# A list-scheduled two-layer backbone: attention products bound into groups, new crossing times for the planner, and one Hyena block moved ahead of the first heads

## The chip, the cores and the metric

The kernel runs on one core of a Trainium2 chip. The metric is device time in microseconds of one execution, as the median over several runs. A separate profiled execution gives the trace that is quoted here.

## The reference

Two layers act on 512 latent and 256 context tokens of width 1024. Each layer is a half-step SwiGLU feed-forward, a token mixing, and a second half-step feed-forward, with layer norms and a modulation computed from the conditioning vectors.

```python
def token_mix(h_lat, h_ctx, w_in, w_out, ...):
    p_lat = h_lat @ w_in
    p_ctx = h_ctx @ w_in
    ...
    oa_l = block_attention(qa_l, concat([ka_c, ka_l]), concat([va_c, va_l]), HEAD_DIM ** -0.5)
    ...
    oc_l = block_attention(qc_l, concat([kc_c, kc_l]), concat([vc_c, vc_l]), (C_NOPE + C_ROPE) ** -0.5)
    ob_l = hyena_mix(pb_l, *hy)
    out_lat = concat([oa_l, ob_l, oc_l]) @ w_out
```

Group A is a grouped-query attention (6 query heads, 2 key heads, width 64), group C a latent attention (6 heads), group B a Hyena convolution with 256 channels. Latent queries read 256 context and 512 latent keys, context queries read context keys. Layer 0 also needs the context outputs, layer 1 only the latent ones.

## The kernel before

**A program that is recorded and then ordered.** The code does not issue instructions directly. A `Recorder` stands in for the engines: `record` notes each operation with its dependencies (from the regions of tiles that it reads and writes), its tiles and a planned `cost`. `order` then runs a list scheduler over all of them: for each of the engines it keeps the operations whose inputs will be there, always takes the engine that can start first, and on it the available operation that comes first in the program. Tile buffers from rotating pools (22 units, 13 weight tiles, 8 banks of PSUM) are handed out in this simulated time too. The result is one fixed order for each engine; on the chip the engines only wait for semaphores. Every instruction of the trace therefore carries one line, L324 (`issue`), and is told apart by tiles and shapes.

**The planner's constants.** `LAT` is what it adds between an operation's planned end and the start of one that depends on it: on the same engine, on another engine, when TensorE is one of the two, and after a DMA. `cost` holds formulas for the duration on each engine. TensorE is also planned at double cost for `WARM` ns after an idle time of more than `IDLE`.

**One step of an attention.** `attend` runs over blocks of 128 queries for two heads at once. It computes scores into PSUM (banks S for the latent keys, C for the context keys), takes row maxima on VectorE, exponentials on ScalarE, sums and a division on VectorE, transposes the weights on TensorE (`turn`), copies the transposes to SBUF on ScalarE (T[0] for the latent keys in two copies, one for each head, then T[1] for the context keys in one) and multiplies values with them. The last part reads

```python
            for i, (k, t, w, c) in enumerate(at):
                for r in range(2):
                    nc.tensor.matmul(o[64 * r:64 * r + 64], vals(h0 + r, k), t[:, w * r + c:w * r + c + 128],
                                     start=i == 0, stop=i == len(at) - 1, tile_position=(0, 64 * r))
```

so that the two heads (r = 0 and 1) fill the two column halves of the array in turn. All of a step's products write one bank `o`, and each one depends on the one before. A latent block has 6 key tiles and so 12 products, a context block 2 key tiles and 4 products. In the trace a product is two recorded matmuls of the form `128*64 128x128`. Layer 0 runs 6 query blocks for 3 pairs of heads in each of the two attentions, layer 1 runs 4. Nothing in the recorder says that a step's products belong together.

**Projections between the heads.** `mix` projects keys, values and queries, transposes them, and splits queries into a high and a low part on ScalarE and VectorE (the `u<-p,u` differences). Then `weave` interleaves the steps of attention A (`heads_a`) with `hy_proj`, a generator that yields after each projection of one Hyena weight block: 24 matmuls for the latent tokens, and in layer 0 as many for the context. A block is followed by a short convolution, one activation on ScalarE and two steps on VectorE (`t<-p,convw,t`) that read the PSUM bank. There are 6 weight blocks. `weave` emits the first block after the first head step; since position in the program is the scheduler's priority, this decides who goes first on each engine where both could go. The weights of a block come by DMA from `in_w_hy` and are split into two parts (`w<-raw` on ScalarE, `w<-raw,w` on VectorE). After attention A follow the Hyena transform, attention C with its own projections woven in, and the output projection.

Of the kernel before, what the change touches and what calls it, by code (L numbers as in the profile page):

```python
# [49 lines left out]
class Recorder:  # L50
# [6 lines left out]
    WRITES = ("out", "accum_out")  # L57
    AHEAD = {"p": 100, "w": 12}
    IDLE, WARM = 3200.0, 3400.0
    LAT = {"same": 130.0, "cross": 180.0, "tensor": 270.0, "dma": 3000.0}  # L60

    def __init__(self, nc):
        self.nc = nc
        self.ops = []
        self.touch, self.first = {}, {}
        self.pools = {}
        for e in ("tensor", "vector", "scalar", "gpsimd", "sync"):
            setattr(self, e, _Engine(self, e))

# [38 lines left out]
    def record(self, eng, method, args, kw):  # L108
# [30 lines left out]
                self.touch[name] = keep  # L139
        self.ops.append((eng, method, args, kw, deps, tiles, self.cost(eng, method, args, kw)))  # L140

    @staticmethod
    def cost(eng, method, args, kw):

        out = args[0]
        n = 1
        for d in out.shape[1:]:
            n *= d
        if eng == "sync":
            b = 4 * n * out.shape[0]  # L150
            return 60.0 + b / 340.0
        if eng == "tensor":
            if method == "transpose":
                return 107.0
            if args[1].dtype != F32:
                return 13.0 + (1.0 if n >= 256 else 4.0) * n / 2.4
            return 13.0 + 4.0 * n / 2.4 * (0.3 if args[1].shape[-1] == 64 and n <= 128 else
                                           min(1.0, args[1].shape[-1] / 128.0))
        ins = [x for x in args[1:] if isinstance(x, bass.AP)]
        psum = any(x.space == PSUM for x in ins)  # L160
        for x in ins:
            m = 1
            for d in x.shape[1:]:
                m *= d
            n = max(n, m)
        small = sum(isinstance(x, bass.AP) for k, x in kw.items() if k in ("bias", "scale", "accum_out"))
        small += sum(isinstance(x, bass.AP) and x.shape[-1] == 1 for x in args[2:])
        if eng == "scalar":
            return (90.0 if not psum else 52.0) + 93.0 * small + 0.833 * n
        if eng == "gpsimd":  # L170
            if method == "tensor_copy":
                return 150.0 + 3.0 * n
            return 130.0 + (3.5 if method == "tensor_scalar" else 2.13) * n
        if method == "reciprocal":
            return 65.0 + 6.3 * n
        fast = method in ("tensor_scalar", "tensor_copy", "memset") and not psum
        return 68.0 + 62.0 * small + (0.52 if fast else 1.04) * n
# [13 lines left out]
    def order(self):  # L191
        ops = self.ops
# [37 lines left out]
        avail = {e: [] for e in when}  # L230
        res = []
        quiet, cold = -1e9, 0.0
        port = {"vector": 0.0, "gpsimd": 0.0}
        shares = [self.shares(*op[:4]) for op in ops]
        starts = self.starts = [0.0] * N

        def offer(n):

            t0 = ready[n]
            for tag, r in opens[n]:  # L240
                if not slots[tag].safe(r):
                    slots[tag].parked[r] = n
                    return
                t0 = max(t0, slots[tag].free[0])
            heapq.heappush(future[ops[n][0]], (t0, n))
# [4 lines left out]
        while len(res) < N:  # L250
            best = None
            for e in when:
                while future[e] and future[e][0][0] <= when[e]:
                    heapq.heappush(avail[e], heapq.heappop(future[e])[1])
                if avail[e]:
                    t0 = when[e]
                elif future[e]:
                    t0 = future[e][0][0]
                else:
                    continue  # L260
                if best is None or t0 < best[0]:
                    best = (t0, e)
            t0, e = best
            when[e] = t0
            while future[e] and future[e][0][0] <= t0:
                heapq.heappush(avail[e], heapq.heappop(future[e])[1])
            n = heapq.heappop(avail[e])
            if shares[n]:
                free = port["gpsimd" if e == "vector" else "vector"]
                if free > t0 + 60.0:  # L270

                    passed = [n]
                    while avail[e] and len(passed) < 12 and shares[avail[e][0]]:
                        passed.append(heapq.heappop(avail[e]))
                    m = heapq.heappop(avail[e]) if avail[e] and not shares[avail[e][0]] else None
                    for x in passed[m is None:]:
                        heapq.heappush(avail[e], x)
                    if m is not None:
                        n = m
            if any(not slots[tag].safe(r) or slots[tag].free[0] > t0 for tag, r in opens[n]):  # L280
                offer(n)
                continue
            wake = []
            for tag, r in opens[n]:
                slots[tag].take(r)
                wake.append(tag)
            res.append(n)
            if shares[n]:
                t0 = max(t0, port["gpsimd" if e == "vector" else "vector"])
                port[e] = t0 + ops[n][6]  # L290
            starts[n] = t0
            end = t0 + ops[n][6]
            if e == "tensor":
                if t0 - quiet > self.IDLE:
                    cold = t0 + self.WARM
                if t0 < cold:
                    end += ops[n][6]
                quiet = end
            when[e] = end
            done = end + (self.LAT["dma"] if e == "sync" else 0.0)  # L300
            for m in succ[n]:
                f = ops[m][0]
                lat = 0.0 if e == f == "tensor" else self.LAT["same" if e == f else "tensor" if "tensor" in (e, f) else "cross"]
                ready[m] = max(ready[m], done + lat)
                need[m] -= 1
                if not need[m]:
                    offer(m)
            for t in ops[n][5]:
                left[t] -= 1
                ends[t] = max(ends.get(t, 0.0), done)  # L310
                if not left[t] and self.pools.get(t) in slots:
                    tag = self.pools[t]
                    slots[tag].give(rank[t], ends[t] + self.LAT["cross"])
                    wake.append(tag)
            for tag in wake:
                for m in slots[tag].woken():
                    offer(m)
# [9 lines left out]
def weave(main, n, side, m):  # L327

    done = 0
    for i, _ in enumerate(main, 1):  # L330
        while done * n < i * m and done < m:
            next(side, None)
            done += 1
    for _ in side:
        pass
# [45 lines left out]
class Core:  # L381
# [617 lines left out]
    def mix(self, l, need_ctx):  # L999
        nc, a, tc = self.nc, self.a, self.tc  # L1000
# [3 lines left out]
        nq = len(qtoks)  # L1004
        streams = ((0, NLT), (NLT, NT)) if need_ctx else ((0, NLT),)
# [74 lines left out]
        for j0, j1 in both:  # L1080
            n = 128 * (j1 - j0)
# [59 lines left out]
        for j0, j1 in streams:  # L1141
            n = 128 * (j1 - j0)
# [64 lines left out]
        def heads_a():  # L1207
            for hp in range(3):
                kept.append(self.unit())
                yield from self.attend(score_a, lambda h, j: Vj(j, 64 * (h // 3), 64 * (h // 3) + 64), 2 * hp, qtoks,  # L1210
                                       hp, kept[hp])

        weave(heads_a(), 3 * nq, hy_proj(), 6 * len(streams))
        for hp in range(3):
            n = 128 * nq
            self.split(self.H[:, hp, :n], self.Hl[:, hp, :n], kept[hp][:, :n])
# [98 lines left out]
        ops = []  # L1315
# [7 lines left out]
    def attend(self, score, vals, h0, qtoks, kt, keep=None):  # L1323

        nc = self.nc
        tt = nc.vector.tensor_tensor
        for j in qtoks:
# [7 lines left out]
            m, z, y = self.small(4), self.small(4), self.small(2)  # L1335
# [30 lines left out]
                turn(p[:, 256 * r:256 * r + 256], r, 512)  # L1366
            nc.scalar.copy(T[1][:, 0:512], p)
            o = self.ps()[:, :128]
            at = [(i, T[0], 512, 128 * i) for i in range(NLT)] if lat else []
            at += [(NLT + i, T[1], 256, 128 * i) for i in range(NT - NLT)]  # L1370
            for i, (k, t, w, c) in enumerate(at):
                for r in range(2):
                    nc.tensor.matmul(o[64 * r:64 * r + 64], vals(h0 + r, k), t[:, w * r + c:w * r + c + 128],
                                     start=i == 0, stop=i == len(at) - 1, tile_position=(0, 64 * r))
            jj = slice(128 * j, 128 * j + 128)
            if keep is None:
                self.split(self.H[:, kt, jj], self.Hl[:, kt, jj], o)
# [259 lines left out]
```

## Time and profile before

| | us |
|---|---|
| median of 3 runs | 2939.81 |
| lowest, highest | 2936.02, 2941.83 |
| the profiled execution | 2944.45 |
| its span, first to last instruction | 2942.3 |
| TensorE busy in it | 2842.6 |

The profiled execution has its own time, which lies a little above the runs' median; its trace is read against that time. Its mean granted TensorE clock is 0.984 of full speed. A matmul's recorded end is modelled and matmuls overlap, so the time that one costs is read from its start to the start of the next. In the timelines, consecutive instructions of one form are merged into one row with their count.

### The profile page before, as it was taken

Reading aid. Unit: us, or ns where it says so; the run is one execution under the profiler, and the core shown is the slowest. Engines: PE = TensorE matmul, PEld = TensorE weight load, DVE = VectorE, ACT = ScalarE, POOL = GpSimd, SP = SyncE. Lnnn points to the kernel's source line nnn. Section 1 sums busy time; section 2 is a strip of 40 time slices with the busy share of each in tenths; the row PEclk is TensorE's granted clock in tenths of the full one; section 3 lists DMA queues with packets and bytes.
Section 4 is the critical chain, followed back from the end, with each engine's and each line's share of the span. In section 5 each row is a group of like instructions: output and inputs, shape, how many; then the busy total and the mean of one; then the engine's idle time right before and its main releaser. Section 6 shows DMA issues by size and latency. Waiting matters only on the chain.

```text
span 2942.3 us, 41183 instructions
## 1 busy us (share of the span) xinstructions
PE 2842.6 (97%) x16132; PEld 2429.0 (83%) x16132; DVE 1713.4 (58%) x3485; ACT 1012.1 (34%) x1988; POOL 558.9 (19%) x545
## 2 busy tenths in 40 slices
PE   7999999999998999999999899999999899799998
PEld 5888888878887799888888788888889687688886
DVE  7887666377577572656536863653267666623335
ACT  4222121255556552121222421212217557432221
POOL 3201223024020031012211220122115120110220
PEclk9999999999999999999999899999999999999999
DMA  8654443122021303343321441431212112123231
GB/s 280 229 158 147 133 136 111 53 90 69 27 68 37 101 30 101 115 129 122 108 93 41 136 143 65 126 101 65 79 63 101 34 58 87 58 87 113 94 107 66
DMA packets 105714, 291.36 MB, mean 99 GB/s; under 512 B 15184, under 2 KB 17392, under 8 KB 105520
## 3 DMA queue, kind: packets, MB, share of 16 engines
q1 hardware_dynamic: 105520, 288.73, 30.3%
q8 instruction: 127, 2.08, 0.3%
q14 instruction: 67, 0.55, 0.1%
HBM read 277.23 MB, written 11.45 MB: 98 GB/s over the span
## 4 chain that ended last, share of the span: by engine, by line
PE 60%; DVE 5%; ACT 2%; issue 1%; POOL 0%; DVEq 0%; ACTq 0%
PE p L324 60%; DVE u L324 2%; DVE s L324 2%; ACT t L324 1%; DVE w L324 1%; DVE t L324 1%; ACT u L324 0%; ACT Hhi L324 0%; ACT w L324 0%; POOL Hlo L324 0%; DVE junk L324 0%; DVE adaw L324 0%; DVE Hlo L324 0%; ACT L324 0%; DVEq L1633 0%
## 5 line engine op out<-in xcount | busy, mean ns | idle before, releaser
L324 PE MATMUL p<-Hhi,w 128*128 128x256 f32 (+1 forms) x5536 | 1367.3, 337 | 8.1 <-ACT Hhi L324 6.1
L324 PEld LDWEIGHTS p<-Hhi,w 128*128 128x128 f32 x5536 | 953.8, 191 | 123.7 <-issue 7.0
L324 PE MATMUL p<-Hlo,w 128*128 128x256 f32 (+1 forms) x2768 | 930.3, 336 | 0.5 <-POOL Hlo L324 0.5
L324 PE MATMUL p<-w,u 128*128 128x512 f32 x2904 | 665.8, 390 | 0.0
L324 PEld LDWEIGHTS p<-w,u 128*128 128x128 f32 x2904 | 543.5, 188 | 111.9
L324 DVE TENSOR_TENSOR w<-raw,w 128x1024 fp32r<-128x1024 f32 (+2 forms) x312 | 389.5, 1249 | 423.1 <-PE p L324 337.6
L324 PEld LDWEIGHTS p<-Hlo,w 128*128 128x128 f32 x2768 | 527.2, 191 | 54.1 <-issue 1.2
L324 ACT CAST w<-raw 128x1024 fp32r<-128x1024 f32 (+2 forms) x312 | 323.0, 1043 | 723.1 <-PE p L324 648.7
L324 POOL TENSOR_TENSOR u<-t,u 128x512 fp32r<-128x512 f32 (+1 forms) x154 | 181.2, 1177 | 1260.3 <-ACT u L324 1141.8
L324 PE MATMUL p<-u,u 128*64 128x128 f32 (+7 forms) x2120 | 299.4, 330 | 20.9 <-ACT t L324 6.1
L324 DVE TENSOR_TENSOR t<-t,p 128x512 f32<-128x512 f32 (+1 forms) x160 | 90.9, 568 | 387.4 <-PE p L324 355.2
L324 PEld LDWEIGHTS p<-u,u 128*64 128x64 f32 (+4 forms) x2120 | 212.3, 162 | 83.7 <-issue 35.7
L324 POOL TENSOR_TENSOR u<-u,t 128x512 f32<-128x512 f32 (+2 forms) x128 | 160.5, 1281 | 524.3 <-DVE t L324 416.0
L324 DVE SCALAR_TENSOR_TENSOR junk<-adaw,crow 128x512 bf16<-128x512 f32 x256 | 207.8, 812 | 74.0 <-PE p L324 46.4
L324 ACT CAST u<-t 128x512 fp32r<-128x512 f32 (+1 forms) x154 | 81.3, 528 | 424.6 <-DVE t L324 424.6
L324 DVE SCALAR_TENSOR_TENSOR adaw<-adaw,crow 128x512 f32<-128x512 f32 x256 | 212.0, 828 | 6.8
L324 PE MATMUL p<-w,Hhi 128*128 128x512 f32 (+3 forms) x712 | 193.8, 355 | 6.9 <-ACT w L324 6.9
L324 DVE TENSOR_TENSOR t<-p,u 128x512 f32<-128x512 f32 x196 | 131.6, 686 | 94.8 <-PE p L324 92.1
L324 ACT ACTIVATE t<-p 128x512 f32<-128x512 f32 (+2 forms) x162 | 79.9, 495 | 293.2 <-PE p L324 287.9
L324 PE MATMUL p<-ident,t 128*128 128x128 f32 x848 | 127.3, 285 | 32.1 <-ACT t L324 17.3
L324 ACT COPY u<-p 128x512 f32<-128x512 f32 (+4 forms) x225 | 112.3, 530 | 94.9 <-PE p L324 93.3
L324 PEld LDWEIGHTS p<-w,Hhi 128*128 128x128 f32 x712 | 129.5, 193 | 18.6 <-ACT w L324 8.0
(122 smaller groups left out, 2174.4 us busy)
## 6 DMA issues: line engine op xcount, KB each, us to landing
raw<-in_ffn_gu SPq DMA_DIRECT2D x176, 512.0 KB, 3.6
adaw<-in_ada_t SPq DMA_DIRECT2D x256, 256.0 KB, 2.9
raw<-in_ffn_down SPq DMA_DIRECT2D x88, 512.0 KB, 3.9
raw<-in_w_out_u SPq DMA_DIRECT2D x16, 512.0 KB, 3.4
u<-in_x_all SPq DMA_DIRECT2D x12, 512.0 KB, 7.7
xs<-u SPq DMA_DIRECT2D x12, 512.0 KB, 2.7
raw<-in_w_hy SPq DMA_DIRECT2D x12, 512.0 KB, 3.4
u<-grow SPq DMA_DIRECT2D x10, 512.0 KB, 4.6
```

Of the source, the lines that this page charges most:

```text
L324: getattr(getattr(self.nc, eng), method)(*args, **kw)
```

## The change

Four edits:

- `bind`, called after a step's products are recorded, gives the first of them every dependency of the group that lies outside it, and notes the group. In `order`, when TensorE's last operation belonged to a group, an available operation of that group is taken before the one that comes first in the program.
- The planner adds `TURN`, 95 ns, to the end of a TensorE operation when the group changes (from none to one and back too).
- `LAT` goes from 180 to 150 ns between engines and from 270 to 200 where TensorE is one of the two; the planned cost of a product goes from 77 to 109 ns.
- In `mix`, the first Hyena weight block (both streams in layer 0) is recorded ahead of the first head step; the other five are woven among the head steps.

No operation is added or removed.

```diff
-    LAT = {"same": 130.0, "cross": 180.0, "tensor": 270.0, "dma": 3000.0}
+    TURN = 95.0
+    LAT = {"same": 130.0, "cross": 150.0, "tensor": 200.0, "dma": 3000.0}
...
+    def bind(self, n0):
+
+        ops = self.ops
+        for n in range(n0, len(ops)):
+            ops[n0][4].update(m for m in ops[n][4] if m < n0)
+            self.group[n] = n0
...
-            return 13.0 + 4.0 * n / 2.4 * (0.3 if args[1].shape[-1] == 64 and n <= 128 else
-                                           min(1.0, args[1].shape[-1] / 128.0))
+            if args[1].shape[-1] == 64 and n <= 128:
+                return 109.0
+            return 13.0 + 4.0 * n / 2.4 * min(1.0, args[1].shape[-1] / 128.0)
...
             n = heapq.heappop(avail[e])
+            if e == "tensor" and tied is not None and self.group.get(n) != tied:
+
+                for m in avail[e]:
+                    if self.group.get(m) == tied:
+                        avail[e].remove(m)
+                        heapq.heapify(avail[e])
+                        heapq.heappush(avail[e], n)
+                        n = m
+                        break
...
                 if t0 < cold:
                     end += ops[n][6]
+                if self.group.get(n) != tied:
+                    end += self.TURN
+                    tied = self.group.get(n)
                 quiet = end
...
-        weave(heads_a(), 3 * nq, hy_proj(), 6 * len(streams))
+        side = hy_proj()
+        for _ in range(len(streams)):
+            next(side)
+        weave(heads_a(), 3 * nq, side, 5 * len(streams))
...
             o = self.ps()[:, :128]
+            n0 = len(nc.ops)
...
+            nc.bind(n0)
```

## Rows read from the trace of the kernel before

**Rows 1.** The page: span, and TensorE's busy time, share and instructions.

```profile
span 2942.3 us, 41183 instructions
...
PE 2842.6 (97%) x16132; PEld 2429.0 (83%) x16132; DVE 1713.4 (58%) x3485; ACT 1012.1 (34%) x1988; POOL 558.9 (19%) x545
```

**Rows 2.** TensorE's waits by releaser: us in total, times, longest us.

```profile
PE p L324 <- ACT t L324: 27.5, 20, 10.3
PE p L324 <- DVE t L324: 10.8, 10, 2.5
...
PE p L324 <- ACT u L324: 9.6, 16, 1.1
PE p L324 <- DVE u L324: 9.0, 12, 1.2
```

**Rows 3.** Stretches: length, engines' busy us, then clock, DMA share, GB/s.

```profile
723.00:741.00 18.00, 13.03 (x49) 8.85 (x48) 16.88 (x37) 11.66 (x32) 2.70 (x3) 0.72 0.20 67
730.00:740.00 10.00, 8.33 (x23) 5.55 (x23) 9.13 (x23) 6.62 (x20) 0.53 (x1) 0.50 0.01 3
741.00:852.00 111.00, 110.82 (x861) 92.30 (x862) 60.95 (x132) 69.67 (x183) 4.04 (x4) 1.00 0.18 57
955.00:1003.00 48.00, 45.09 (x344) 35.61 (x345) 25.42 (x67) 32.89 (x91) 0.00 (x0) 0.89 0.37 122
2298.00:2350.00 52.00, 42.36 (x308) 31.89 (x307) 31.83 (x70) 36.03 (x97) 1.28 (x1) 0.93 0.06 19
2460.00:2485.00 25.00, 19.78 (x137) 16.04 (x136) 18.19 (x39) 16.65 (x46) 0.00 (x0) 0.86 0.29 90
```

**Rows 4.** Groups by form on TensorE: count, busy us, mean ns, idle before.

```profile
L324 PE MATMUL p<-w,u 128*128 128x512 f32 x2904 | 665.8, 390 | 0.0
...
L324 PE MATMUL p<-u,u 128*64 128x128 f32 x1248 | 102.2, 287 | 2.0 <-ACT t L324 1.0 <-ACT u L324 0.9
```

**Rows 5.** TensorE's timeline around cut product groups: start us, length us.

```profile
741.80 0.43 PE L324 MATMUL p<-u,u 128*64 128x128 f32 x2
...
754.91 0.43 PE L324 MATMUL p<-u,u 128*64 128x128 f32 x2
755.28 0.73 PE L324 MATMUL p<-Hhi,w 128*128 128x512 f32 x2
755.85 0.39 PE L324 MATMUL p<-Hlo,w 128*128 128x512 f32 x1
756.17 1.52 PE L324 MATMUL p<-u,u 128*64 128x128 f32 x22
757.62 0.50 PE L324 MATMUL p<-Hhi,w 128*128 128x512 f32 x1
...
2510.61 0.43 PE L324 MATMUL p<-u,u 128*64 128x128 f32 x2
```

**Rows 6.** TensorE's timeline around a product group left whole.

```profile
2480.44 0.65 PE L324 MATMUL p<-ident,t 128*128 128x128 f32 x4 [0.68 <-ACT u L324]
2481.64 1.53 PE L324 MATMUL p<-u,u 128*64 128x128 f32 x24 [0.55 <-ACT t L324]
2483.10 1.09 PE L324 MATMUL p<-ident,t 128*128 128x128 f32 x8
```

**Rows 7.** ScalarE's timeline there: copies of the transposes.

```profile
2479.80 0.59 ACT L324 COPY u<-p 128x512 f32<-128x512 f32 x1 [0.75 <-PE p L324]
...
2481.48 0.58 ACT L324 COPY u<-p 128x512 f32<-128x512 f32 x1
```

**Rows 8.** VectorE's timeline before and in 723 to 741 us.

```profile
710.34 5.05 DVE L324 TENSOR_TENSOR w<-raw,w 128x1024 fp32r<-128x1024 f32 x3
...
732.00 0.75 DVE L324 SCALAR_TENSOR_TENSOR t<-p,convw,t 128x511 f32<-128x511 f32 x1
...
734.32 0.48 DVE L324 SCALAR_TENSOR_TENSOR t<-p,convw,t 128x255 f32<-128x255 f32 x1
```

**Rows 9.** TensorE's timeline at the end of that stretch.

```profile
734.95 3.33 PE L324 MATMUL p<-u,u 128*128 128x256 f32 x10 [0.92 <-DVE t L324]
```

More of the change, by code (lines that the diff above doesn't have):

```diff
@@ L66, in __init__ @@
         self.pools = {}
+        self.group = {}
         for e in ("tensor", "vector", "scalar", "gpsimd", "sync"):
@@ L232, in order @@
         quiet, cold = -1e9, 0.0
+        tied = None
         port = {"vector": 0.0, "gpsimd": 0.0}
```

## The prediction

> **What bounds the kernel now.** I read the page's busy shares first. TensorE is busy for 2842.6 of the 2942.3 us of the profiled span [rows 1]: nothing that does not shorten TensorE's own work, or fill its waits, can move the end. Next come TensorE's waits. The four classes that end inside the mixing stages or at their borders, on the exponentials and copies of ScalarE and on VectorE's differences and conversions, add up to 27.5 + 10.8 + 9.6 + 9.0 = 56.9 us in 58 waits [rows 2]. The third view is a table of stretches [rows 3]. The first attention of layer 0 (741 to 852 us) has TensorE busy for 110.82 of 111 us: a microsecond of TensorE saved there is a microsecond of the kernel. Four other stretches of the attentions are not full: 723 to 741 us (13.03 of 18 us, clock 0.72), 955 to 1003 us (45.09 of 48, clock 0.89), 2298 to 2350 us (42.36 of 52) and 2460 to 2485 us (19.78 of 25, clock 0.86). There the softmax chain or a bank of PSUM that is not yet free holds TensorE up.
>
> A stretch that is "full" can still hold loss, since a matmul that starts late counts as busy. So I compared starts with starts in the timeline. A projection matmul of 128x512 takes 665.8 / 2904 = 0.229 us from start to start [rows 4]; that is what a step costs when nothing is switched.
>
> **What a cut product group costs.** One step of `attend` ends in 12 products (24 recorded matmuls with 64 output columns) for a latent query block, or 4 (8 recorded) for a context block: layer 0 has 36 groups, layer 1 has 24, 48 of 24 and 12 of 8, which gives the 1248 of the row [rows 4]. In the order of the trace these 60 groups stand in pieces: 38 times a first product alone (2 recorded matmuls), from 741.80 to 2510.61 us, with the rest later [rows 5]; 7 more cuts lie elsewhere in a group (16 and 8 above all). That makes 45 cuts, counted in the order of TensorE's instructions.
>
> The price of one cut of the first kind, from the group at 754.91 us [rows 5]: the lone product holds TensorE from 754.91 to 755.28, 0.37 us; the remaining 22 from 756.17 to 757.62, 1.45 us; together 1.82 us. A group left whole, at 2481.64 us, takes until 2483.10, 1.46 us [rows 6]. So 0.36 us is lost inside the group, because the two column halves run beside each other only when their products alternate, and the cut shifts that pattern. Outside it, the three projection matmuls between the pieces last from 755.28 to 756.17, 0.89 us, where three unswitched ones take 3 x 0.229 = 0.69: 0.20 us for one way out of the 64-column form and back. A cut costs 0.36 + 0.20 = 0.56 us. For the seven others I charge the 0.20 alone, the part that every cut has. Sum: 38 x 0.56 + 7 x 0.20 = 22.7 us of TensorE time.
>
> As a bound from above: all 64-column records are busy for 102.2 us, and 48 x 1.53 [rows 6] plus 12 x 0.56 (a third of 1.46 and the same tail of 0.07, an estimate from the same rows) would be 80.2. That leaves 22.0 us inside the groups, where my count has 38 x 0.36 = 13.7; with 45 x 0.20 outside it is 31.0 us. Some of the difference is the overlapping tail of each piece, and products at the low clock, so 22.7 stays my figure and 31 the bound.
>
> The Trainium skill, TensorEngine Tiling (Array Packing), Tiling Modes (Key Properties), says that a change of tiling mode, though not of the tile within one, drains TensorE. The trace agrees on the border cost, 0.20 us for the two switches, but by the rule alone the 0.36 us inside the group would not exist; that case is the third rival below.
>
> **The change part by part.** *Binding.* `bind` gives the first product all outside dependencies of its group, and `order` prefers the group's other products once it has begun. Each depends only on the one before, so none of the 45 cuts can remain. I take three quarters of the 22.7 us, 17 us (estimate: most cuts lie in stretches where TensorE is full, but some in the four that are not, where the saved time partly turns into waiting): -17, ends 0 and -31.
>
> The added wait: the first product must now wait for the copy of the last transposes, which it did not need. In the group of rows 6 the transposes start at 2480.44, the last copy on ScalarE runs from 2481.48 for 0.58 us [rows 7], and the first product starts at 2481.64. Bound, it could start at 2481.48 + 0.58 + 0.05 = 2482.11 (0.05 being 2480.44 less the end of the copy before, 2479.80 + 0.59), 0.47 us later. Queued behind it on TensorE are the next group's scores and transposes; but the order is chosen by the planner, which puts other ready work in front, a projection or the next scores, so in full stretches it costs nothing. Cover is missing in the stretches that are not full, some 12 of the 48 groups: 12 x 0.47 = +5.6, taken as +5. If no cover existed anywhere it would be 48 x 0.47 = +22.6.
>
> *The Hyena block in front.* The first block of `hy_proj` now stands ahead of the first head in the program, so its convolution on VectorE outranks the head's reductions, and the other blocks move up a place. The same matmuls run. In layer 0, TensorE already executes that block before the heads, but three of its conversion steps on VectorE come only from 732.00 to 734.32 us [rows 8], and hold two PSUM banks till then; a wait of 0.92 us ends on the last [rows 9]. At stake is the stretch 723 to 741 us: 18 - 13.03 = 4.97 us idle, and the 10 us at half clock from 730 us on; of those 10 us 8.33 are busy at a clock of 0.50 [rows 3], so with the clock up about 4 us less; together 9 us. The filler exists: the weights of the next block are ready by 715.39 us [rows 8]. Against it, VectorE is busy for 16.88 of these 18 us [rows 3], and the conversions put first (0.75 and twice about 0.48 us and one more of the first kind that already runs early) delay the queries' differences by up to 2.5 us. I take -4, ends -9 and +3. In layer 1, four blocks already run before the heads; I take 0, and for its emptier tail up to +5.4 us, one block of 24 matmuls at 0.229.
>
> *Crossing times and costs.* These constants alter no instruction, only the order. `cost` gives a copy of 512 columns from PSUM 52 + 0.833 x 512 = 479 ns, and with the old crossing of 270 the planner sees 749 ns until TensorE follows, with the new one 679; the trace shows 2480.44 - 2479.80 = 640 [rows 6, 7]. The new figure is nearer. A product costs 1.46 / 12 = 0.12 us against a planned 0.077 before and 0.109 now. Better figures should help, but a list schedule answers to small shifts in either direction: 58 waits [rows 2] of 0.07 us more or less are 4 us. I take 0, ends -5 and +5. No DMA is added, and the transfers' order on SyncE's queue changes only with the planner's; no wait of these four classes names one.
>
> **Sum.** -17 + 5 - 4 + 0 = -16 us. The profiled execution took 2944.45 us (span 2942.3 and 2.15 around it); it would be 2928. The median of the runs, 2939.81, lies 4.6 below that execution, so the forecast is 2939.8 - 16 = 2924 us.
>
> **Rivals.**
> 1. *The gain goes back into waiting* (no measurable change). For: in four stretches TensorE waits for the softmax chain, not for itself. Against: most cuts lie in full stretches such as 741 to 852 us. With half of 22.7 realized, the wait of +5 and no gain from the Hyena block: -6 us or less, 2934 to 2945, chance 0.17.
> 2. *The bound product's wait decides* (slower). The place is the copy of the last transposes ahead of each group of 24. If ScalarE serves the next head's exponentials first, a group waits for a whole exponential (0.58 us is the copy; one of 512 takes about as long), 0.47 + 0.6 = 1.07 us; over 48 groups 51 us against 22.7 + 4 saved is +24, 2964 at worst. It decides from 33 us, that is from 31 of 48 groups without cover on; the slower case ends at 2946 to 2964. Its likeliest time is 2950. For: a wait long enough also drops the clock, as at 730 to 740 us. Against: only some 12 groups lie where TensorE is not full. Chance 0.13.
> 3. *Only the switches are saved* (the rule named above, alone): 45 x 0.20 = 9 us, with the +5 and -4 a gain of 8 us, 2932. Against: 1.82 against 1.46 us in the rows. Chance 0.08; still faster.
> 4. *More than forecast:* all 22.7 us, no added wait, -9 in the Hyena stretch: -32, 2908. Chance 0.12.
>
> **How the numbers follow.** The forecast (2912 to 2933) has 0.50. A difference of 0.2%, 5.9 us, is about what a measurement of this kernel can tell from none. Faster: 0.50 + 0.08 + 0.12 = 0.70; the same 0.17; slower 0.13. For eight in ten the range goes from 2906, which takes in the fourth rival, to 2943, which takes in most of the first, and leaves out the slower one.
>
> **What would show it.** Right: the 64-column records' busy time falls from 102.2 towards 80 us; they stand in runs of 24 and 8; 741 to 852 us becomes some 10 us shorter with TensorE still full; the stall at 723 to 741 us shrinks and its half-clock stretch with it. Wrong: the groups are whole, but new waits on ScalarE's copies stand before them, or TensorE's waits in the later heads of layer 1 grow because the Hyena blocks are used up; or the borders outside the attentions, reordered by the new constants, change by more than the 5 us allowed.

## The result and the profile after

The changed kernel takes 2904.1 us (median of 4 runs, 2903.6 to 2904.9) against 2939.65 us before: a ratio of 0.9881, interval 0.9863 to 0.9898. It gained 35.5 us where 16 were forecast, more than the range of 2906 to 2943 held, and close to the fourth rival's 2908. The profiled execution took 2903.62 us, 40.8 less than the one before. That one lay 4.6 us above its median, so some 5 us of the difference between the two traces is the spread between executions.

The page of the changed kernel, to be read beside [rows 1]:

```profile
span 2901.2 us, 41228 instructions
...
PE 2812.3 (97%) x16132; PEld 2416.2 (83%) x16132; DVE 1716.4 (59%) x3485; ACT 1006.4 (35%) x1988; POOL 566.3 (20%) x545
```

The span fell by 41.1 us. TensorE's busy time fell by 30.3 with the same 16132 matmuls, and its idle time by the remaining 10.8. So most of the gain is time in which TensorE counted as busy already.

The groups by form of the changed kernel, beside [rows 4]:

```profile
L347 PE MATMUL p<-w,u 128*128 128x512 f32 x2904 | 665.7, 390 | 0.0
...
L347 PE MATMUL p<-u,u 128*64 128x128 f32 x1248 | 82.0, 280 | 0.8 <-ACT u L347 0.7
```

The projections cost the same to 0.1 us; the products' busy time fell from 102.2 to 82.0, near the 80 that whole groups were estimated to take. The timeline of TensorE, beside [rows 5]:

```profile
747.28 0.82 PE L347 MATMUL p<-ident,t 128*128 128x128 f32 x6
748.03 1.53 PE L347 MATMUL p<-u,u 128*64 128x128 f32 x24
749.49 0.88 PE L347 MATMUL p<-ident,t 128*128 128x128 f32 x6
```

All 60 groups are whole. A group of 24 lasts 1.46 us from its start to the start of what follows (748.03 to 749.49). No idle time stands in front of this group: the transposes of another step run there. Ahead of all products together TensorE idles for 0.8 us, the last figure of their row above, where it was 2.0 us before.

TensorE's waits after the change, beside [rows 2]:

```profile
PE p L347 <- ACT t L347: 26.6, 20, 10.3
...
PE p L347 <- DVE u L347: 6.2, 9, 1.3
...
PE p L347 <- ACT u L347: 4.5, 11, 0.7
...
PE p L347 <- DVE t L347: 3.7, 7, 0.9
```

The class that the added wait belongs to, `ACT u` (ScalarE's copies), did not grow by 5 us; it fell from 9.6 to 4.5. `DVE t` fell from 10.8 to 3.7. Which edit brought that down is read from the experiments. Stretches after the change, beside [rows 3]:

```profile
723.00:741.00 18.00, 15.36 (x88) 12.19 (x87) 17.47 (x34) 11.95 (x30) 4.22 (x5) 1.00 0.30 96
730.00:740.00 10.00, 7.96 (x49) 6.63 (x47) 9.66 (x20) 6.88 (x17) 1.80 (x2) 1.00 0.16 52
743.30:838.70 95.40, 94.93 (x804) 81.48 (x804) 56.74 (x126) 65.23 (x177) 2.03 (x2) 1.00 0.18 56
```

In 723 to 741 us the clock is at its full level (1.00 against 0.72) and TensorE runs 88 matmuls where it ran 49; it is still idle for 2.6 of the 18 us. The third row is the whole of the first attention's products: from the first product to the start of the last it now takes 94 us (743.29 to 837.26), where it took 108 (741.80 to 850.13). Not all of these 14 us are saved: the trace shows 27 matmuls of 512 columns and 24 of 256 fewer between these two points, work of a Hyena block that now runs earlier. At 0.229 and 0.12 us each that is about 9 us, an estimate from their starts. With the binding alone, where 844 matmuls stand there against 849 before, the stretch takes 101 us.

VectorE and TensorE in that stretch, beside [rows 8] and [rows 9]; the first fence is VectorE, the second TensorE:

```profile
726.19 2.19 DVE L347 SCALAR_TENSOR_TENSOR t<-p,convw,t 128x511 f32<-128x511 f32 x4
```

```profile
728.85 0.40 PE L347 MATMUL p<-Hlo,w 128*128 128x512 f32 x1
729.08 0.62 PE L347 MATMUL p<-Hhi,w 128*128 128x512 f32 x2
...
732.78 0.28 PE L347 MATMUL p<-Hhi,w 128*128 128x256 f32 x1
```

All four convolution steps of the first block now run from 726.19 us on; before, three of them ran at 732 to 734. The second block's matmuls follow (latent tokens at 729, context tokens from 733) and fill what had been a stall. That they take the banks which these steps free is argued from the order; the trace does not name the banks.

### The profile page after: what moved, and what is told of

Read it like the earlier page. It is cut to its first block, busy times and chain, and to the rows that moved or that the text cites. A ratio compares the mean times of both kernels' runs of the same rounds, so it can differ in the third digit from the quotient of the medians.

```text
span 2901.2 us, 41228 instructions
## 1 busy us (share of the span) xinstructions
PE 2812.3 (97%) x16132; PEld 2416.2 (83%) x16132; DVE 1716.4 (59%) x3485; ACT 1006.4 (35%) x1988; POOL 566.3 (20%) x545
## 4 chain that ended last, share of the span: by engine, by line
PE 63%; DVE 5%; ACT 2%; issue 1%; POOL 0%; DVEq 0%; ACTq 0%; POOLq 0%
PE p L347 63%; DVE u L347 2%; DVE s L347 2%; ACT t L347 1%; DVE w L347 1%; DVE t L347 1%; ACT u L347 0%; ACT Hhi L347 0%; ACT w L347 0%; DVE Hlo L347 0%; DVE junk L347 0%; DVE adaw L347 0%; POOL Hlo L347 0%; ACT L347 0%; DVEq L1661 0%
## 5 line engine op out<-in xcount | busy, mean ns | idle before, releaser
L347 PE MATMUL p<-u,u 128*64 128x128 f32 (+7 forms) x2120 | 277.4, 323 | 19.3 <-ACT t L347 5.2
L347 PEld LDWEIGHTS p<-u,u 128*64 128x64 f32 (+4 forms) x2120 | 202.8, 160 | 69.7 <-issue 27.0
L347 PE MATMUL p<-w,Hhi 128*128 128x416 f32 (+3 forms) x712 | 194.0, 354 | 6.7 <-ACT w L347 6.7
L347 POOL TENSOR_TENSOR Hlo<-t,Hhi 128x512 fp32r<-128x512 f32 x72 | 95.5, 1336 | 244.5 <-ACT Hhi L347 244.3
```

What stands on the lines that cost most here:

```text
L347: getattr(getattr(self.nc, eng), method)(*args, **kw)
```

## The experiments

Four theories for the part of the gain beyond the cuts: (A) the binding itself also takes waits and low clock away; (B) the new crossing times; (C) the Hyena block; (D) chance, since a list schedule reorders under any disturbance.

**Each edit alone on the kernel before** (median before in these runs: 2938.7 us).

The binding alone:

```diff
+            n0 = len(nc.ops)
...
+            nc.bind(n0)
```

> The kernel before with the binding of the products alone; crossing times, costs and the Hyena blocks as before. Every theory says that the 45 cuts go, some 20 us of TensorE. Theory A (binding also takes the waits and the low clock away, because whole groups shorten the chain and hold PSUM banks for less time): -30 to -36 us, 2904 to 2910. Theory B (the rest comes from the new crossing times): about -18 us, 2922. Theory C (the rest comes from the Hyena block in front): about -18 us, 2922, with the stall before the first products of layer 0 as before. Theory D (any new order of a list schedule moves the time by some 10 us by chance): anywhere from 2910 to 2930.

Measured: 2911.75 us, ratio 0.991 (0.9893 to 0.9927), -27 us. Its products by form, two classes of TensorE's waits, and two stretches:

```profile
L346 PE MATMUL p<-u,u 128*64 128x128 f32 x1248 | 80.3, 277 | 0.8 <-ACT u L346 0.7
```

```profile
PE p L346 <- ACT u L346: 6.8, 14, 0.9
...
PE p L346 <- DVE t L346: 5.0, 7, 1.8
```

```profile
723.00:741.00 18.00, 13.36 (x53) 9.44 (x52) 16.85 (x36) 11.55 (x30) 2.72 (x3) 0.72 0.21 67
...
955.00:1003.00 48.00, 48.00 (x359) 40.28 (x358) 26.51 (x58) 30.34 (x73) 3.52 (x2) 1.00 0.39 132
```

The stall at 723 us is still there at a clock of 0.72; but 955 to 1003 us, which had 45.09 us busy at 0.89, is full at 1.00. Theory A is the nearest, a little short of it; the run without the binding, below, decides against it.

The crossing times alone:

```diff
-    LAT = {"same": 130.0, "cross": 180.0, "tensor": 270.0, "dma": 3000.0}
+    LAT = {"same": 130.0, "cross": 150.0, "tensor": 200.0, "dma": 3000.0}
```

> The kernel before with the new crossing times alone (150 and 200 ns). Theory B: -12 to -18 us, 2922 to 2928, with fewer waits of TensorE in the attentions and the cuts still there. Theories A and C: within 4 us of 2940. Theory D: 2930 to 2950.

Measured: 2941.75 us, ratio 1.0014 (1.0004 to 1.0023), +3 us. Theory B falls.

The Hyena block alone:

```diff
-        weave(heads_a(), 3 * nq, hy_proj(), 6 * len(streams))
+        side = hy_proj()
+        for _ in range(len(streams)):
+            next(side)
+        weave(heads_a(), 3 * nq, side, 5 * len(streams))
```

> The kernel before with the first Hyena block ahead of the first heads alone. Theory C: -12 to -18 us, 2922 to 2928, the 18 us stretch before the first products of layer 0 full and at the full clock. Theories A and B: within 4 us of 2940. Theory D: 2930 to 2950.

Measured: 2935.44 us, ratio 0.9988 (0.9979 to 0.9997), -3 us. The stretch is at the full clock as theory C has it, though not full, and the whole is worth little; theory C's 12 to 18 us fall:

```profile
723.00:741.00 18.00, 15.76 (x90) 12.41 (x88) 17.42 (x34) 11.88 (x28) 3.99 (x4) 1.00 0.29 96
```

The cost of a product alone:

```diff
+            if args[1].shape[-1] == 64 and n <= 128:
+                return 109.0
```

> The kernel before with the planned cost of a product at 109 ns instead of 77 alone. Theories A, B and C: within 4 us of 2940, since the constant orders little. Theory D: 2930 to 2950, as far off as the other single edits without a reason of its own.

Measured: 2933.83 us, ratio 0.9983 (0.9974 to 0.9992), -5 us. It is larger than the Hyena block's; none of theories A to C has a reason for it.

**Each edit taken out of the changed kernel** (median before in these runs: 2938.8 us).

```diff
-            nc.bind(n0)
```

> The changed kernel without the binding (the call is left out, so no group exists and no switch is planned); crossing times, product cost and Hyena order new. Theory A: within 5 us of the kernel before, 2935 to 2945, the cuts back. Theory B or C: keeps 12 to 18 us of the gain, 2922 to 2928. Theory D: 2925 to 2950.

Measured: 2928.96 us, ratio 0.9966 (0.9954 to 0.9978). The products are back at 101.0 us:

```profile
L347 PE MATMUL p<-u,u 128*64 128x128 f32 x1248 | 101.0, 283 | 1.2 <-ACT u L347 0.9
```

So the binding is worth 24.9 us in the company of the others, and the others without it 9.8. The time lies in the range of theory D alone, just above that of B and C and well under theory A's. The page, two classes of TensorE's waits and two stretches of this run:

```profile
span 2926.7 us, 41241 instructions
...
PE 2835.3 (97%) x16132; PEld 2422.4 (83%) x16132; DVE 1717.9 (59%) x3485; ACT 1009.6 (34%) x1988; POOL 565.9 (19%) x545
```

```profile
PE p L347 <- ACT u L347: 5.7, 11, 0.8
...
PE p L347 <- DVE t L347: 1.7, 3, 0.9
```

```profile
845.00:1600.00 755.00, 748.43 (x4372) 646.95 (x4369) 443.68 (x858) 253.00 (x511) 136.96 (x110) 1.00 0.27 86
955.00:1003.00 48.00, 47.21 (x345) 38.81 (x344) 24.76 (x57) 30.70 (x76) 2.54 (x2) 1.00 0.43 154
```

Without the binding, the two classes are already down to 5.7 and 1.7 us, and the clock is at its full level from 845 to 1600 us. Adding the binding shortens the span by 25.5 us, of which 23.0 is TensorE's busy time and 2.5 its idle time; the mean granted clock of the profiled execution is 0.987 with and without it. In this trace 43 first products stand alone. At 0.56 us each they make 24.1 us, nearly all of the 24.9: in company the binding gains by the cuts, not by waits or clock.

```diff
-    LAT = {"same": 130.0, "cross": 150.0, "tensor": 200.0, "dma": 3000.0}
+    LAT = {"same": 130.0, "cross": 180.0, "tensor": 270.0, "dma": 3000.0}
```

> The changed kernel with the old crossing times (180 and 270 ns). Theory A or C: within 4 us of the changed kernel, 2900 to 2908. Theory B: 2916 to 2922. Theory D: 2895 to 2920.

Measured: 2903.2 us, ratio 0.9878 (0.9861 to 0.9894): the same as the changed kernel. The crossing times give nothing.

```diff
-        side = hy_proj()
-        for _ in range(len(streams)):
-            next(side)
-        weave(heads_a(), 3 * nq, side, 5 * len(streams))
+        weave(heads_a(), 3 * nq, hy_proj(), 6 * len(streams))
```

> The changed kernel with the Hyena blocks woven as before. Theory A or B: within 4 us of the changed kernel, 2900 to 2908. Theory C: 2916 to 2922, the stall ahead of the first products of layer 0 back at 5 us of idle time and 10 us of half clock. Theory D: 2895 to 2920.

Measured: 2912.1 us, ratio 0.9909 (0.9894 to 0.9924): the block is worth 8 us here, where alone it was worth 3. The stall is back:

```profile
723.00:741.00 18.00, 11.88 (x48) 8.80 (x47) 15.75 (x32) 10.76 (x28) 2.70 (x3) 0.73 0.20 66
```

```diff
-            if args[1].shape[-1] == 64 and n <= 128:
-                return 109.0
...
-    TURN = 95.0
+    TURN = 0.0
```

(with the old factor of 0.3 for the product's cost)

> The changed kernel with the product planned at 77 ns and no planned switch (TURN 0). Theories A, B and C: within 4 us of the changed kernel, 2900 to 2908. Theory D: 2895 to 2920.

Measured: 2908.6 us, ratio 0.9899 (0.9884 to 0.9914): the two planned costs are worth 4.5 us.

**What a cut costs, and the bank** (median before: 2939.5 us; for the fourth, 2939.3).

```diff
-            nc.bind(n0)
+            nc.bind(n0 + 1)
```

> The changed kernel with the first product of each group left free and only the others bound: the first may start before the last copy, the rest stay whole. In the planned order 45 first products stand alone again, in 43 places more than in the changed kernel. If a cut costs what the rows of before said, 0.56 us on a full TensorE: 43 x 0.56 = +24 us, 2928. If the rows over-counted, or the time was waiting that the earlier start fills: under +12 us, 2904 to 2916. If binding gains more than the cuts (theory A, by the bank of PSUM or the clock): +28 us or more, over 2932.

Measured: 2928.0 us, ratio 0.9962 (0.9949 to 0.9975), 23.9 us over the changed kernel. In the trace 45 first products stand alone, and the products come in 99 pieces, 43 more than in the changed kernel (groups that follow each other directly count as one piece): 0.56 us for each added piece. Products and one cut, by form and in the timeline:

```profile
L347 PE MATMUL p<-u,u 128*64 128x128 f32 x1248 | 99.9, 279 | 0.5 <-ACT u L347 0.4
```

```profile
752.02 0.43 PE L347 MATMUL p<-u,u 128*64 128x128 f32 x2
752.39 0.73 PE L347 MATMUL p<-Hhi,w 128*128 128x512 f32 x2
...
753.50 1.52 PE L347 MATMUL p<-u,u 128*64 128x128 f32 x22
754.96 1.31 PE L347 MATMUL p<-ident,t 128*128 128x128 f32 x10
```

The piece of 2 lasts 0.37 us and that of 22 lasts 1.46, as in [rows 5]. The price of a cut of this kind was right.

```diff
+            n1 = len(nc.ops)
             for r in range(2):
                 turn(p[:, 256 * r:256 * r + 256], r, 512)
-            nc.scalar.copy(T[1][:, 0:512], p)
             o = self.ps()[:, :128]
+            nc.ops[n1 + 1][5].add(o.tensor.name)
+            nc.scalar.copy(T[1][:, 0:512], p)
```

> The changed kernel with the products still whole, but the plan takes their PSUM bank from the step's transposes of the context keys on, about 1 us earlier, as the lone first product did. If the later bank is why waits and low clock fell with the binding: +5 to +12 us, 2909 to 2916. If it is only that the pieces are whole: within 4 us of 2904.

Measured: 2916.7 us, ratio 0.9924 (0.9909 to 0.9939), +12.6 us. A middle length, from the copy on:

```diff
-            nc.scalar.copy(T[1][:, 0:512], p)
             o = self.ps()[:, :128]
+            nc.scalar.copy(T[1][:, 0:512], p)
+            nc.ops[-1][5].add(o.tensor.name)
```

> The changed kernel with whole groups, the plan taking their PSUM bank from the copy of the last transposes on ScalarE, between the changed kernel (at the first product) and the run that took it from the transposes (+12.6 us). If the time follows the length of the hold: +3 to +8 us, 2907 to 2912. If only a hold across the transposes matters: within 2 us of 2904.

Measured: 2908.95 us, ratio 0.9901 (0.9884 to 0.9918), +4.8 us. One class of TensorE's waits, in the run from the transposes and in the run from the copy:

```profile
PE p L347 <- DVE t L347: 10.6, 13, 2.5
```

```profile
PE p L347 <- DVE t L347: 8.3, 9, 1.9
```

It was 3.7 us in the changed kernel. The longer the plan holds the bank, the longer TensorE waits. That PSUM is short in these stretches is argued from this: no run counted free banks, and the smaller step, 4.8 us, is no larger than edits of a planner constant gave.

**Disturbances and two further versions.**

```diff
-    LAT = {"same": 130.0, "cross": 180.0, "tensor": 270.0, "dma": 3000.0}
+    LAT = {"same": 130.0, "cross": 180.0, "tensor": 265.0, "dma": 3000.0}
```

> The kernel before with the crossing time at TensorE planned as 265 ns instead of 270: a change without any meaning, to see how far the time moves when a list schedule is only disturbed. If the single edits of 3 to 5 us (crossing times +3, Hyena block -3, product cost -5) are chance, this moves by as much, 3 to 6 us either way; if they are effects, it stays within 2 us of 2939.

Measured: 2939.4 us, ratio 1.000 (0.9991 to 1.001). The changed kernel disturbed in the same way:

```diff
-    LAT = {"same": 130.0, "cross": 150.0, "tensor": 200.0, "dma": 3000.0}
+    LAT = {"same": 130.0, "cross": 150.0, "tensor": 205.0, "dma": 3000.0}
```

> The changed kernel with the crossing time at TensorE planned as 205 ns instead of 200, the same disturbance on this side. Chance: 3 to 6 us off 2904 either way. Effects: within 2 us of 2904.

Measured: 2901.9 us, ratio 0.9873 (0.9859 to 0.9888), -2.2 us. Two disturbances, 0 and 2 us: theory D is too small for the binding, but the 3 us of a single edit are not far above it.

```diff
-        for _ in range(len(streams)):
+        for _ in range(2 * len(streams)):
             next(side)
-        weave(heads_a(), 3 * nq, side, 5 * len(streams))
+        weave(heads_a(), 3 * nq, side, 4 * len(streams))
```

> The changed kernel with the first two Hyena blocks ahead of the first heads instead of one. If the block in front gains because its conversions free their banks sooner, a second gains again where the wait remains: -2 to -6 us, 2898 to 2902. If it was the stretch before the first products alone, which is already cured: 0 to +6 us, 2904 to 2910, since the later heads have fewer blocks.

Measured: 2908.5 us, ratio 0.9894 (0.9879 to 0.9909), +4 us: one block cures the stretch, a second gains nothing more and costs 4 us.

```diff
+            n0 = len(nc.ops)
             for r in range(2):
                 score(S[r], Cr[:, r], h0 + r, j)
+            for n in range(n0, len(nc.ops)):
+                nc.ops[n0][4].update(m for m in nc.ops[n][4] if m < n0)
```

> The changed kernel with the outside dependencies of a step's scores also gathered on the first of them. If partly begun steps hold banks for nothing: -2 to -6 us, 2898 to 2902. If the scores' inputs are there anyway: within 2 us of 2904.

Measured: 2912.2 us, ratio 0.9907 (0.9892 to 0.9921), +8 us. Gathering dependencies is no good in itself; it pays where a cut has a price. Why it costs 8 us here was not followed up.

## Why the prediction fell short

**The cuts: number and place right, the share taken of them wrong.** 45 cuts at 22.7 us of TensorE time were forecast. The products' busy time fell by 20.2 us in the changed kernel, the time lost at the borders comes on top, and setting 45 first products free cost 23.9 us, the 24 that the rows of before gave. The sum took three quarters, 17 us, on the ground that some cuts lay in stretches that were not full. That step failed: practically all of it came. In the trace of before only 7 of the 38 lone products lie in those four stretches, and four of the seven stand 12 to 38 us behind TensorE's last wait and 80 us or more ahead of the next.

**What the price is made of: read wrongly in part.** The prediction put the 0.36 us inside a group down to the two column halves falling out of step, and charged the seven other cuts 0.20 us. A group of before that was cut between pairs of products, into 16 and 8 records, shows otherwise:

```profile
789.23 1.09 PE L324 MATMUL p<-u,u 128*64 128x128 f32 x16
790.26 0.73 PE L324 MATMUL p<-Hhi,w 128*128 128x512 f32 x2
790.83 0.39 PE L324 MATMUL p<-Hlo,w 128*128 128x512 f32 x1
791.06 0.40 PE L324 MATMUL p<-Hhi,w 128*128 128x512 f32 x1
791.38 0.66 PE L324 MATMUL p<-u,u 128*64 128x128 f32 x8
791.97 0.50 PE L324 MATMUL p<-Hhi,w 128*128 128x512 f32 x1
```

Its pieces take 1.03 and 0.59 us, 1.62 together and 0.16 more than a whole group, though the halves alternate in both. The four projections between them take 1.12 us against 4 x 0.229 = 0.92, again 0.20 more. So each extra piece costs about 0.16 us at its end and 0.20 at its borders, 0.36 in all. Only the remaining 0.20 of the 0.56 is peculiar to a first product that runs without its partner: the 11 products after it take 1.45 us [rows 5], as long as 12. Priced so, the cuts of before come to about 38 x 0.56 + 7 x 0.36 = 23.8 us, an estimate.

**The added wait of +5 us: wrong.** The forecast charged 12 groups with 0.47 us. With all groups whole, TensorE idles for 0.8 us ahead of the products altogether, and its waits on ScalarE's copies did not grow with the binding: from 9.6 to 6.8 us with the binding alone, from 5.7 to 4.5 in company. The planner knows of the wait and puts other work in front, in thin stretches too. Together the binding was put at -12 us and measured at -27 alone and -24.9 in company: these two terms make most of the error. That `order` prefers a begun group decides nothing: planned without that preference, the changed kernel gives the same program, so the gathered dependencies do it all.

**Waits and low clock are not where the binding's gain lies.** With the binding alone, 955 to 1003 us went from a clock of 0.89 to 1.00, which looks like a gain beyond the cuts. But that stretch is at 1.00 too in the run with the other three edits and no binding, and in company the cuts cover the gain. Alone, the binding's 27 us are some 3 more than the cuts at their price; what these 3 us are is not settled. A PSUM bank taken later is a cause that could act so (+12.6 us when the plan takes it from the transposes on), but the run with free first products, whose bank is taken earlier too, lost no more than its cuts cost. That the binding acted by the bank is therefore not shown.

**The Hyena block: mechanism right, size inside its ends.** Forecast -4, ends -9 and +3; measured -3 alone, -8 in company. Conversions went ahead, the next block filled most of the stretch, and the clock held, as the sum had it. The run without the block alone, with the clock at 0.73 again, shows cause and place.

**The constants: 0 forecast, ends -5 and +5.** The crossing times gave +3 alone and nothing in company; the planned costs of product and switch -5. Together that is within the ends, on the good side. Why the planned costs help is not known: a change of 5 ns in the changed kernel's crossing time alone moved it by 2 us. The nearer crossing figures did not help, so their nearness to the trace was no argument.

**The drain rule.** The Trainium skill, TensorEngine Tiling (Array Packing), Tiling Modes (Key Properties), says that a change of tiling mode drains TensorE. The third rival priced that at the two switches alone, 0.20 us a cut and 9 us in all. The trace decides against this price: 0.56 us a cut, as the run with free first products shows. Whether the 0.16 us that an extra piece costs at its end is part of such a drain, no run here shows.

**Slower** did not come near: for that the wait would have had to stand uncovered before 31 of 48 groups, and no such wait was found. Singly the four edits sum to -27 + 3 - 3 - 5 = -32 us; the whole is -35.5.

## What to carry to other kernels

Small products that use the array's column halves in turn should be issued as one run. Here a cut cost 0.56 us where it left a product without its partner and about 0.36 us between pairs, and a full TensorE hid it, because late starts count as busy. Read starts against starts, count the cuts, and do not discount the sum for cover that has not been measured. When several edits go together, take each out as well as putting each in alone: the waits and the clock that fell with the binding alone fell without it too. A new constant of a planner should be timed alone, however well it agrees with the trace.

## What the runs showed that was not expected

When the plan held a single PSUM bank from the transposes on for each step, the kernel took 12.6 us longer, without any change in the work; when it held the bank from the copy after them on, 4.8 us, which is no more than a planner constant gave. Raising the planned cost of a product from 77 to 109 ns, with nothing else changed, gave 5 us.
